# Gates of the latents with seven products for eight, 512-wide conditioning sums and more gates made ahead, in a two-layer mixer trunk

## The chip, the cores and the metric

The kernel runs on one core of a Trainium2 chip. A time is the device time of one execution in microseconds (us). It is given as the median of repeated executions; one more execution is profiled. In the profile PE is TensorE (PEld its weight loads), DVE is VectorE, ACT is ScalarE, POOL is GpSimd and SP is SyncE, which issues the DMAs here.

## The reference

Two layers work on 1024 latent tokens and 256 context tokens of width 1024. Each layer modulates its input by a conditioning vector, projects it to 5632 columns, runs three token mixers (Fourier, gating unit, windowed attention), and merges their projections with sigmoid gates. The last 3072 columns of the projection are the gates.

```python
s_c = jax.nn.silu(c)
for l in range(DEPTH):
    shift, scale, gate = jnp.split(s_c @ w_ada[l] + b_ada[l], 3, axis=-1)
    h = _rms(x) * (1.0 + scale[:, None, :]) + shift[:, None, :]
    fa, za, u, vs, zb, q, k, va, zc, g = _split_proj(h @ w_in[l])
    ...
    ya = _fourier(fa) * jax.nn.silu(za)
    yb = _sgu(u, vs, w_s, b_s) * jax.nn.silu(zb)
    yc = attn * jax.nn.silu(zc)
    ga, gb, gc = jnp.split(jax.nn.sigmoid(g), N_BRANCHES, axis=-1)
    merged = ga * (ya @ w_pa) + gb * (yb @ w_pb) + gc * (yc @ w_pc)
    x = x + gate[:, None, :] * (merged @ w_out[l])
```

Context tokens go through the same steps with a conditioning vector of their own. In the second layer only their keys and values are needed, so there the gates exist for the latents alone. All data is float32.

## The kernel before

**Numbers.** Every float32 operand of a product is split into a high part, rounded to the matmul's format by ScalarE, and a low part, the rest, taken by VectorE. A product is then three matmuls: high by high, high by low, low by high (`mm3`). Operands lie channels on partitions, tokens or columns along the free dimension. `granule` loads a weight tile of up to 128x1024 (`raw`, two buffers) and makes its halves `whi` and `wlo` (five buffers each), one operation of ScalarE (L212) and one of VectorE (L213) per tile.

**Groups.** Tokens are in three groups: "C" (256 of the context), "0" and "1" (512 latents each). `H[g]` holds the layer's modulated input of a group, as eight k blocks of 128 channels with high and low part.

**Stages.** Per layer: attention, Fourier mixing, the gating unit (`sgu`), the gates, the output projection. Projections that do not depend on a stage run in it as fillers (`Fill`), so that TensorE has work: `products` makes the branch projections by `w_pa` and `w_pc` and stages them to DRAM (`S["P", ...]`), and `ahead` makes some gate blocks early and stages their tanh to DRAM (`S["T", ...]`).

**Gates.** `gates` goes through eight column blocks j of 128. For each branch b and group g it multiplies the 128 columns of the gate weights with `H[g]` over all eight k blocks (24 matmuls of 128x512), takes the tanh on ScalarE (L734, into one of the two `ta` buffers), and merges: VectorE computes (tanh + 1) times the branch's projection (L681 for the first branch, L684 for the others, into one of two `tb` buffers), and GpSimd adds it to the column's sum `m` (L685). The branch projection comes from DRAM through `lp`, or, for the middle branch, straight from PSUM: the products by `w_pb` are made here. Merged columns go to DRAM and come back as operands of the output projection.

**Conditioning sums.** The products of the conditioning vectors with `w_ada` for the gate columns of this layer and for the next layer run on VectorE in the gates stage (`ada_dve`): for each item of 256 columns, eight k blocks and one or two vectors, a multiply-add over 128x256 (L196, the first one L192), and at the end small matmuls with a column of ones. `keep_in_program_order` holds the first of them in place.

**Order.** Each engine works through its own list in order. A scheduler makes the lists from the program; the order in which the program is written is a priority, and buffers (`bufs=`) set how far one step can run ahead of another.

## Time and profile before

| | |
|---|---|
| median of three executions | 1948.63 us (1947.56 to 1950.77) |
| profiled execution | 1947.46 us |
| its span, first to last instruction | 1945.7 us |
| mean granted TensorE clock | 0.992 |
| TensorE busy | 1888.2 us, 97% |
| VectorE, ScalarE, GpSimd busy | 1083.1, 798.4, 610.6 us |
| stage of the gates, layer 0 and layer 1 | about 690 to 985 and 1630 to 1858 us |

The span is less than the time of the execution, because starting and ending lie around it. Rows of the profile give a line of the program, the engine, the operation, the tiles it writes and reads (out<-in), and the shape. A row with [.. <-X] tells how long the engine idled before it and what ended the wait. In a table of stretches each engine has its busy time and its count of instructions; in a row of waits stand the total, the number and the longest.

### The profile page before, as it was taken

To read this page: it belongs to the slowest core of one execution; us is meant where nothing else is said; L and a number is where in the kernel's file an instruction comes from. 1 tells how busy PE (TensorE), PEld (TensorE's weight loads), DVE (VectorE), ACT (ScalarE), POOL (GpSimd) and SP (SyncE) were. 2 spreads that over 40 slices of the span, in tenths; PEclk is the share of its full clock that TensorE was granted. 3 is DMA by queue.
4 is the path that set the end of the run, shared out by engine and by line. 5 is a ranking of instruction groups with operands and counts; after the bars stand their busy time and mean duration, and the time that the engine had idled before them with its cause. 6 is when DMAs were issued, how large, how long until landed. Compare 5 with 4: busy or idle time off the path is not lost.

```text
span 1945.7 us, 31000 instructions
## 1 busy us (share of the span) xinstructions
PE 1888.2 (97%) x10975; PEld 1639.1 (84%) x10975; DVE 1083.1 (56%) x2175; ACT 798.4 (41%) x2088; POOL 610.6 (31%) x975
## 2 busy tenths in 40 slices
PE   7889999999999999999999989999999999999998
PEld 2888999999988887888878978899888888888887
DVE  4565665556655548766355556666665655622242
ACT  2654555445644422111243445555554443111221
POOL 1564344443231112121124454334432021211122
PEclk9999999999999999999999999999999999999999
DMA  9332122213554667554374412112124568633362
GB/s 331 105 101 64 50 68 61 72 47 95 162 185 152 191 214 244 164 171 148 120 259 152 136 55 66 57 59 84 34 87 152 155 194 264 201 93 98 127 220 103
DMA packets 270610, 259.77 MB, mean 134 GB/s; under 512 B 20792, under 2 KB 213496, under 8 KB 270456
## 3 DMA queue, kind: packets, MB, share of 16 engines
q1 hardware_dynamic: 270456, 257.80, 41.9%
q8 instruction: 86, 1.41, 0.3%
q14 instruction: 68, 0.56, 0.1%
HBM read 196.91 MB, written 60.83 MB: 132 GB/s over the span
## 4 chain that ended last, share of the span: by engine, by line
PE 82%; DMA 6%; DVE 5%; ACT 3%; issue 2%; POOL 2%; SPq 1%; POOLq 0%; ACTq 0%; DVEq 0%
PE mm L237 16%; PE mm L238 16%; PE mm L239 16%; PE s L238 6%; PE s L237 6%; PE s L239 6%; PE pt L399 3%; DMA raw<-in_w_in_dram 2%; PE o L407 2%; PE o L406 2%; PE s L371 2%; PE s L364 1%; PE s L365 1%; DVE wlo L213 1%; DMA lt<-dT 1%
## 5 line engine op out<-in xcount | busy, mean ns | idle before, releaser
L213 DVE TENSOR_TENSOR wlo<-raw,whi 128x1024 fp32r<-128x1024 f32 (+2 forms) x210 | 243.3, 1161 | 216.3 <-ACT whi L212 207.5
L212 ACT CAST whi<-raw 128x1024 fp32r<-128x1024 f32 (+2 forms) x210 | 202.7, 967 | 363.7 <-PE s L238 139.2
L237 PE MATMUL mm<-hh,whi 128*128 128x512 f32 (+1 forms) x752 | 292.4, 389 | 5.6 <-DVE st L562 3.8
L238 PE MATMUL mm<-hl,whi 128*128 128x512 f32 (+1 forms) x752 | 291.1, 387 | 0.0
L239 PE MATMUL mm<-hh,wlo 128*128 128x512 f32 (+1 forms) x752 | 290.7, 387 | 0.0
L237 PE MATMUL mm<-whi,hh 128*128 128x256 f32 (+1 forms) x704 | 217.6, 309 | 8.1 <-DVE qt L447 5.2
L685 POOL TENSOR_TENSOR m<-m,tb 128x512 f32<-128x512 f32 x64 | 87.1, 1363 | 412.0 <-DVE tb L684 367.6
L239 PE MATMUL mm<-whi,hl 128*128 128x256 f32 (+1 forms) x704 | 214.7, 305 | 0.0
L238 PE MATMUL mm<-wlo,hh 128*128 128x256 f32 (+1 forms) x704 | 214.7, 305 | 0.0
L237 PEld LDWEIGHTS mm<-hh,whi 128*128 128x128 f32 x752 | 141.3, 188 | 33.3 <-DVE st L562 4.7
L239 PEld LDWEIGHTS mm<-hh,wlo 128*128 128x128 f32 x752 | 141.3, 188 | 27.3
L238 PEld LDWEIGHTS mm<-hl,whi 128*128 128x128 f32 x752 | 141.4, 188 | 25.6
L237 PEld LDWEIGHTS mm<-whi,hh 128*128 128x128 f32 x704 | 135.5, 192 | 14.7 <-issue 5.6
L387 POOL TENSOR_SCALAR P<-P,rd 128x640 f32<-128x640 f32 (+2 forms) x144 | 115.0, 809 | 102.1 <-DVE rd L385 63.9
L238 PEld LDWEIGHTS mm<-wlo,hh 128*128 128x128 f32 x704 | 135.7, 193 | 5.0
L239 PEld LDWEIGHTS mm<-whi,hl 128*128 128x128 f32 x704 | 135.4, 192 | 4.8
L238 PE MATMUL s<-hl,whi 128*128 128x512 f32 x352 | 137.5, 391 | 0.0
L237 PE MATMUL s<-hh,whi 128*128 128x512 f32 x352 | 137.4, 390 | 0.0
L239 PE MATMUL s<-hh,wlo 128*128 128x512 f32 x352 | 137.2, 390 | 0.0
L269 DVE TENSOR_TENSOR pl<-pt,ph 128x512 fp32r<-128x512 f32 (+1 forms) x184 | 112.0, 615 | 27.4 <-ACT ph L268 25.0
L268 ACT CAST ph<-pt 128x512 fp32r<-128x512 f32 (+1 forms) x184 | 95.8, 535 | 28.0 <-PE o L406 15.8
L196 DVE SCALAR_TENSOR_TENSOR aacc<-araw,scol,aacc 128x256 f32<-128x256 f32 x196 | 102.2, 554 | 5.1 <-DMA araw<-in_w_ada_dram 2.7
(303 smaller groups left out, 4435.0 us busy)
## 6 DMA issues: line engine op xcount, KB each, us to landing
raw<-in_w_in_dram SPq DMA_DIRECT2D x122, 512.0 KB, 4.1
araw<-in_w_ada_dram SPq DMA_DIRECT2D x48, 512.0 KB, 6.0
raw<-in_w_out_dram SPq DMA_DIRECT2D x40, 512.0 KB, 3.8
dP<-st SPq DMA_DIRECT2D x64, 256.0 KB, 2.3
lp<-dP SPq DMA_DIRECT2D x64, 256.0 KB, 4.2
x<-in_x_dram SPq DMA_DIRECT2D x16, 512.0 KB, 8.6
raw<-in_w_pc_dram SPq DMA_DIRECT2D x32, 256.0 KB, 2.9
dM<-m SPq DMA_DIRECT2D x32, 256.0 KB, 3.4
```

Source lines behind the costliest of these rows:

```text
L196: DVE.scalar_tensor_tensor(acc[:, v, :], raws[k // 4][:, k % 4, :], sc, acc[:, v, :], ALU.mult, ALU.add)
L212: ACT.copy(hi, raw)
L213: DVE.tensor_tensor(lo, raw, hi.bitcast(F32), ALU.subtract)
L237: PE.matmul(o, lh, rh, start=start, stop=False)
L238: PE.matmul(o, lh, rl, start=False, stop=False)
L239: PE.matmul(o, ll, rh, start=False, stop=stop)
L268: ACT.copy(hi, src)
L269: DVE.tensor_tensor(lo, src, hi.bitcast(F32), ALU.subtract)
L371: PE.matmul(bc[:, h * 256:h * 256 + 256], qt[:, s, 2 * pr + h, :], kk[:, g, SEQ:NTOK], start=(h + s == 0), stop=(s == 1), skip_group_check ...
L387: POOL.tensor_scalar(P[hh][:, :nl + 256], P[hh][:, :nl + 256], rd[:, hh:hh + 1], 1.0, ALU.mult, ALU.mult)
L399: PE.transpose(b[:, (2 * i + hh) * 128:(2 * i + hh + 1) * 128], P[hh][:, (i0 + i) * 128:(i0 + i + 1) * 128], ident)
L685: POOL.tensor_tensor(m, m, s, ALU.add)
```

## The change

**Seven products for eight.** For each pair of columns j = 2p, 2p+1 and branch b, the gates of both latent groups are a 2x2 block product: the weights in two k halves by two columns (a11, a12 for the first column, a21, a22 for the second), the inputs in two k halves by two token groups (B11, B21 for "0", T1's source and B22 for "1"). The code takes seven half-k products of 12 matmuls with combinations of the weights (s1 to s4) and of the inputs (T1 to T4), and sums them in PSUM where that is possible; x2, x3, x5 are partial results that ScalarE copies out. s1 is made by VectorE, s2 to s4 by GpSimd (L757), one late sum by VectorE (L828), another by GpSimd (L840). 18 pairs are made so, ten in layer 0 and eight in layer 1.

**Differences.** T1 to T4 are made once per layer (`differences`), ahead of the gates, T1 in the place of B12. The fillers beside them are four late gate blocks and the products by `w_pb`, which now go to DRAM too.

**Merging.** It reads the branch projections of all three branches from DRAM. The context's two columns are merged as one tile of 512; all of the context's merged columns go to DRAM. The order of the output groups in layer 0 is "0", "C", "1".

**Conditioning sums.** `ada_steps` works on one k block of 512 columns at a time. The layer's own gate columns are summed under the gating unit, the next layer's in layer 0's gates, one step after each of the first products.

**Casts.** `operand` makes halves of 512 columns from a raw tile that is always 1024 wide (ten buffers each).

**Gates ahead.** Eight blocks in layer 0 and sixteen in layer 1 are made ahead of their merging, where before it was four and eight.

```diff
-    def ada_dve(l, jb, nv, pool):
...
+    def ada_steps(items, pool):
...
+        def block(l, jb, nv, k, acc):
+            raw = pool.tile([128, 512], F32, "araw", bufs=2)
+            nc.sync.dma_start(raw, a["w_ada"][l, k * 128:(k + 1) * 128, jb * 128:jb * 128 + 512])
+
+            def sums():
+                if k == 0:
+                    acc.extend(tb() for _ in range(nv))
                 for v in range(nv):
                     sc = scol[:, k, v:v + 1]
                     if k == 0:
+                        ins = DVE.tensor_scalar(acc[v], raw, sc, None, ALU.mult)
                     else:
+                        ins = DVE.scalar_tensor_tensor(acc[v], raw, sc, acc[v], ALU.mult, ALU.add)
+                    if v == 0:
+                        tc.keep_in_program_order(ins)
...
+    def operand(src, n=512):
+
+        hi = wp.tile([128, 512], F32R, "whi", bufs=10)[:, :n]
+        lo = wp.tile([128, 512], F32R, "wlo", bufs=10)[:, :n]
+        ACT.copy(hi, src)
+        DVE.tensor_tensor(lo, src, hi.bitcast(F32), ALU.subtract)
+        return hi, lo
...
+    def differences(tpool):
...
+        def steps():
+            for k in range(KC // 2):
+                for t, x, y in ((T3, B22, B12), (B12, B12, B11), (T2, B22, B12), (T4, B21, T2)):
+                    d = ta()
+                    POOL.tensor_tensor(d, x[0][k].bitcast(F32), y[0][k].bitcast(F32), ALU.subtract)
+                    e = tb()
+                    DVE.tensor_tensor(e, x[1][k].bitcast(F32), y[1][k].bitcast(F32), ALU.subtract)
+                    DVE.tensor_tensor(d, d, e, ALU.add)
+                    split(t[0][k], t[1][k], d)
+                    yield
...
+        def times(o, A, B, start):
+            for k in range(KC // 2):
...
+                PE.matmul(o, A[0][:, c], B[0][k], start=start and k == 0, stop=False, skip_group_check=True)
+                PE.matmul(o, A[0][:, c], B[1][k], start=False, stop=False, skip_group_check=True)
+                PE.matmul(o, A[1][:, c], B[0][k], start=False, stop=last, skip_group_check=True)
+            next(sums, None)
...
+        def add(m, b, t, pp):
             if b == 0:
                 DVE.scalar_tensor_tensor(m, t, 1.0, pp, ALU.add, ALU.mult)
             else:
-                s = tb(n)
-                DVE.scalar_tensor_tensor(s, t, 1.0, pp, ALU.add, ALU.mult)
-                POOL.tensor_tensor(m, m, s, ALU.add)
...
+                DVE.scalar_tensor_tensor(pp, t, 1.0, pp, ALU.add, ALU.mult)
+                POOL.tensor_tensor(m, m, pp, ALU.add)
...
+                if ("T", b, js[0], "0") in S:
+                    for g in lat:
+                        for j in js:
+                            t = ta()
+                            nc.sync.dma_start(t, S["T", b, j, g])
+                            merge(j, g, t, True)
+                    continue
...
+                A = operand(a11)
+                times(z, A, B11, True)
+                ACT.copy(x, z)
+                s1 = combined(DVE, a21, a22, ALU.add)
+                A = operand(s1)
+                times(y, A, T1, True)
+                x5 = copy("x5", y)
+                s2 = combined(POOL, s1, a11, ALU.subtract)
+                A = operand(s2)
+                times(z, A, T2, False)
+                x2 = copy("x2", z)
+                A = operand(a12)
+                times(x, A, B21, False)
...
+                s4 = combined(POOL, a12, s2, ALU.subtract)
+                s3 = combined(POOL, a11, a21, ALU.subtract)
...
+                times(z, A, T3, False)
+                x3 = copy("x3", z)
+
+                def p3():
+                    A = operand(s4)
+                    times(y, A, B22, False)
+                    DVE.tensor_tensor(x2, y, x2, ALU.add)
+                    merge(js[0], "1", x2)
+
+                def p4():
+                    A = operand(a22)
+                    times(z, A, T4, False)
...
+                POOL.tensor_tensor(x3, x3, x5, ALU.add)
+                merge(js[1], "1", x3)
...
-        blocks = [(b, 0, g) for b in (0, 2) for g in lat]
+        pairs = [(b, p) for p in range(2 if last else 1) for b in (0, 2)]
+        blocks = [(b, 2 * p + i, "1") for b, p in pairs for i in range(2)]
+        late = [(b, j, "0") for b, j, _ in blocks[-4:]]
...
+        sums = ada_steps(ada, sp)
         for i, _ in enumerate(sgu(l, groups, sp, S, yb)):
+            for x in range(2):
+                next(sums, None)
+                fill.upto((i + (x + 1) / 2) * whole / (units // 128))
...
+        sevens, combos = differences(tpool)
+        fill = Fill(ahead(l, late[:2], S, st), products(l, groups, yb, 2, "w_pb", 1, S, st, True), ahead(l, late[2:], S, st))
+        for i, _ in enumerate(combos):
+            fill.upto((i + 1) * (16 * units + 2048) / 16)
+        fill.rest()
...
+        gates(l, groups, S, [] if last else [(l + 1, j, 2) for j in (8, 0, 12, 4)], A, sevens)
```

**The order on VectorE.** The scheduler's list for VectorE inside layer 0's gates, before the change (L196 and L192 are the sums, L213 a low half of weights, L269 one of `w_pb`, L684 a merge):

```order
L192 TENSOR_SCALAR aacc_9346<-araw,scol 128x256 x2
L196 SCALAR_TENSOR_TENSOR aacc_9346<-araw,scol,aacc_9346 128x256 x3
L684 SCALAR_TENSOR_TENSOR tb<-ta,pt 128x512
L684 SCALAR_TENSOR_TENSOR tb<-ta,lp_9484 128x512
L196 SCALAR_TENSOR_TENSOR aacc_9346<-araw,scol,aacc_9346 128x256
L269 TENSOR_TENSOR pl<-praw,ph 128x512
L196 SCALAR_TENSOR_TENSOR aacc_9346<-araw,scol,aacc_9346 128x256 x6
L213 TENSOR_TENSOR wlo<-raw,whi 128x1024
```

And after it, around the combination s1 (L757) of the fourth pair (L193 are the sums, L223 low halves, L762 and L764 merges, L828 the late sum x2):

```order
L762 SCALAR_TENSOR_TENSOR m_10243<-x_10392,lp 128x512
L193 SCALAR_TENSOR_TENSOR tb<-araw,scol,tb 128x512
L757 TENSOR_TENSOR sw<-raw 128x512
L193 SCALAR_TENSOR_TENSOR tb<-araw,scol,tb 128x512
L762 SCALAR_TENSOR_TENSOR m_10242<-ta,lp 128x512
L193 SCALAR_TENSOR_TENSOR tb<-araw,scol,tb 128x512
L764 SCALAR_TENSOR_TENSOR lp<-ta,lp 128x512
L223 TENSOR_TENSOR wlo<-sw,whi 128x512
L193 SCALAR_TENSOR_TENSOR tb<-araw,scol,tb 128x512
L828 TENSOR_TENSOR x_10531<-s,x_10531 128x512
```

Between the making of s1 and its low half, which is the operand of the second product, the list now has two sums and two merges, and the merges take their tanh and projection from tiles in SBUF.

**The order on GpSimd.** Before the change, its list in the same stage holds only the additions of the merging:

```order
L685 TENSOR_TENSOR mC<-mC,tb 128x256 x2
L685 TENSOR_TENSOR m_9107<-m_9107,tb 128x512
L685 TENSOR_TENSOR m_9108<-m_9108,tb 128x512
L685 TENSOR_TENSOR m_9107<-m_9107,tb 128x512
L685 TENSOR_TENSOR m_9108<-m_9108,tb 128x512
```

After it (L757 are s2, s4 and s3, L840 is x3, L765 the additions of the merging):

```order
L757 TENSOR_TENSOR sw<-sw,raw 128x512
L765 TENSOR_TENSOR m_9973<-m_9973,lp 128x512
L757 TENSOR_TENSOR sw<-raw,sw 128x512
L765 TENSOR_TENSOR m_9974<-m_9974,lp 128x512
L757 TENSOR_TENSOR sw<-raw 128x512
L765 TENSOR_TENSOR m_9975<-m_9975,lp 128x512
L840 TENSOR_TENSOR x_10392<-x_10392,x_10302 128x512
```

The combinations that TensorE's operands are made from now alternate with the additions, in one list.

More of the change, by code (lines that the diff above doesn't have):

```diff
@@ new lines, in sums @@
+                    if v == 0:
+                        tc.keep_in_program_order(ins)
+                if k == KC - 1:
+                    pa = bank("o")
+                    for i in range(4):
+                        for v in range(nv):
+                            PE.matmul(pa[:, 2 * i + v:2 * i + v + 1], acc[v][:, i * 128:(i + 1) * 128], ones[:, 0:1], start=True, stop=True)
+                    for i in range(4):
+                        DVE.tensor_scalar(adac[l][:, jb + i, 0:nv], pa[:, 2 * i:2 * i + nv], bada[l][:, jb + i:jb + i + 1], None, ALU.add)
@@ new lines, in block @@
+            return sums
+        for l, jb, nv in items:
+            acc = []
+            for k in range(KC):
+                if len(todo) == 2:
+                    todo.pop(0)()
+                todo.append(block(l, jb, nv, k, acc))
+                yield
+        for f in todo:
+            f()
+            yield
+    def operand(src, n=512):
[4 more added lines that the diff above has]
+        return hi, lo
@@ new lines, in raw_weights, with part @@
+    def raw_weights(src, shape):
+        raw = wp.tile([128, 1024], F32, "raw", bufs=2)
+        n = shape[1] * shape[2]
+        nc.sync.dma_start(raw[:, :n].rearrange("p (k c) -> p k c", k=shape[1]), src)
+        return raw[:, :n]
+    def granule(src, shape):
+        raw = raw_weights(src, shape)
+        n = shape[1] * shape[2]
+        return [operand(raw[:, c:min(c + 512, n)], min(512, n - c)) for c in range(0, n, 512)]
+    def part(w, width, k, c0=0, n=None):
+        c = k * width + c0
+        x = c // 512
+        c -= x * 512
+        return [y[:, c:c + (n or width)] for y in w[x]]
@@ L615, in gated_u @@
                     yield 2 * n
-        lead = context_blocks(range(9, 12)) if "C" in groups else [(b, 2, "0") for b in (0, 2)]
+        lead = context_blocks(range(9, 12)) if "C" in groups else [(2, j, "0") for j in range(2)]
         return ([ahead(l, lead, S, st), silus("Z", C_ZC, (2, 3)), silus("A", C_ZA, (0, 1))] + [rows(l, groups, "F", C_FA, S, st)],
@@ L624, in before_work @@
             return ahead(l, context_blocks(range(9)), S, st)
-        return ahead(l, [(b, 1, "0") for b in (0, 2)], S, st, CTX)
+        return ahead(l, [(0, j, "0") for j in range(2)], S, st, CTX)
     def few(gen, n):
@@ L669, in products, with half_blocks, new @@
                 yield n * nkb
-    def gates(l, groups, S, ada, side, yb):
-        mp = Pool(tc, name="mp", bufs=1, side=side)
-        zq = Pool(tc, name="zq", bufs=1, side=side)
-        lat = [g for g in groups if g != "C"]
-        hC = new_h("C") if "C" in groups else None
-        todo = []
-        def add(m, b, t, n, pp):
+    def half_blocks(g, i):
+        return [H[g][x][4 * i:4 * i + 4] for x in range(2)]
+    def differences(tpool):
+        def new(tag):
+            ts = [tpool.tile([128, KC // 2, 512], F32R, f"{tag}{x}") for x in "hl"]
+            return [[t[:, k, :] for k in range(KC // 2)] for t in ts]
+        B11, B12, B21, B22 = (half_blocks(g, i) for i in range(2) for g in ("0", "1"))
+        T2, T3, T4 = new("t2"), new("t3"), new("t4")
+        def steps():
[7 more added lines that the diff above has]
+                    split(t[0][k], t[1][k], d)
+                    yield
+        return (B11, B21, B22, B12, T2, T3, T4), steps()
@@ L743, in gates @@
+        for k in (KC - 2, KC - 1):
+            merged("0", k, mp, "araw", 2)
         mp.close()
@@ L922, in out_phase @@
         wt[0] = w_half(a["w_out"][l], 0)
-        if order[0] != "C":
-            operands(order[0])
+        operands(order[0])
         load(order[0])
@@ L983, in trunk_kernel @@
         groups = ["0", "1"] if last else ["C", "0", "1"]
-        ada = [(l, j, 1 if last else 2) for j in range(16, 24, 2)]
-        if not last:
-            ada += [(l + 1, j, 2) for j in range(0, 16, 2)]
+        ada = [(l, j, 1 if last else 2) for j in (16, 20)]
         S = {}
```

208 lines of the change are left out of this document (98 added, 110 removed).

## The prediction

> **What bounds the kernel now.** I read the page's first and fourth parts, then a table of stretches, then the two timelines that show VectorE and GpSimd next to each other, and the waits.
>
> ```profile
> span 1945.7 us, 31000 instructions
> PE 1888.2 (97%) x10975; PEld 1639.1 (84%) x10975; DVE 1083.1 (56%) x2175; ACT 798.4 (41%) x2088; POOL 610.6 (31%) x975
> PE 82%; DMA 6%; DVE 5%; ACT 3%; issue 2%; POOL 2%; SPq 1%; POOLq 0%; ACTq 0%; DVEq 0%
> ```
>
> TensorE is busy 97% of the span and carries 82% of the chain that ended last: matmuls bound the kernel, and whatever takes matmuls away pays, as long as nothing else rises above what is left. The profiled execution took 1947.46 us, 1.76 more than its span and 0.06% under the median of the runs, 1948.63. Whether something else rises is a question for the stages that are edited. Of the stretches below, the columns are the bounds in us, the length, then busy time and count of PE, PEld, DVE, ACT and POOL, the granted clock, the DMA share and GB/s. In order they are layer 0's gating unit with the products of `w_pa`, layer 0's gates, the same two of layer 1, 100 us inside the last, and 3.4 us that the clock argument needs.
>
> ```profile
> core 0: us, PE busy (x) PEld busy (x) DVE busy (x) ACT busy (x) POOL busy (x), PEclk, DMA share, GB/s
> 616.00:690.00 74.00, 70.68 (x347) 58.71 (x347) 42.67 (x76) 33.64 (x77) 17.28 (x30) 0.98 0.63 195
> 690.00:985.00 295.00, 292.44 (x1359) 242.61 (x1358) 184.43 (x344) 66.55 (x102) 56.53 (x48) 1.00 0.58 178
> 1545.00:1630.00 85.00, 83.37 (x381) 67.67 (x380) 44.66 (x71) 36.19 (x73) 13.69 (x24) 1.00 0.62 194
> 1630.00:1858.00 228.00, 227.27 (x1007) 187.44 (x1006) 93.75 (x128) 54.75 (x80) 43.49 (x32) 1.00 0.49 155
> 1750.00:1850.00 100.00, 100.00 (x442) 82.58 (x441) 26.71 (x34) 23.25 (x34) 13.74 (x11) 1.00 0.35 113
> 628.70:632.10 3.40, 3.40 (x10) 2.43 (x10) 3.40 (x7) 2.44 (x5) 1.73 (x3) 0.50 0.50 150
> ```
>
> The fifth gives the price of a matmul: 100.00 / 442 = 0.226 us from start to start for 128x512. A product of 12 (half of k, three matmuls each) is 2.71 us, the seven of a pair 19.0. In the first four rows PE idles 3.3, 2.6, 1.6 and 0.7 us, 8.2 in all. In layer 0's gates VectorE and GpSimd are busy 184 + 57 us of 295. That looks like room, but the two timelines show that they don't run side by side.
>
> ```profile
> 735.10 1.78 DVE L681 SCALAR_TENSOR_TENSOR m<-ta,lp 128x512 f32<-128x512 f32 x1
> 736.80 0.68 DVE L684 SCALAR_TENSOR_TENSOR tb<-lt,lp 128x512 f32<-128x512 f32 x1
> 737.40 0.47 DVE L196 SCALAR_TENSOR_TENSOR aacc<-araw,scol,aacc 128x256 f32<-128x256 f32 x1
> 737.80 1.77 DVE L681 SCALAR_TENSOR_TENSOR m<-ta,lp 128x512 f32<-128x512 f32 x1
> 750.83 0.68 DVE L684 SCALAR_TENSOR_TENSOR tb<-ta,lp 128x512 f32<-128x512 f32 x1
> 751.43 1.52 DVE L196 SCALAR_TENSOR_TENSOR aacc<-araw,scol,aacc 128x256 f32<-128x256 f32 x1
> 752.88 1.77 DVE L269 TENSOR_TENSOR pl<-praw,ph 128x512 fp32r<-128x512 f32 x1
> ```
>
> And GpSimd's of the same stretch:
>
> ```profile
> 735.00 1.33 POOL L685 TENSOR_TENSOR m<-m,tb 128x512 f32<-128x512 f32 x1 [3.02 <-DVE tb L684]
> 737.56 1.46 POOL L685 TENSOR_TENSOR m<-m,tb 128x512 f32<-128x512 f32 x1 [1.23 <-DVE tb L684]
> 750.99 3.11 POOL L685 TENSOR_TENSOR m<-m,tb 128x512 f32<-128x512 f32 x2 [3.85 <-DVE tb L684]
> ```
>
> The merge begun on VectorE at 735.10 ends at 736.88, 0.55 after GpSimd's addition ended (735.00 + 1.33 = 736.33); the next one ends at 739.57, again 0.55 after GpSimd (739.02). Undisturbed such an operation takes 0.68 and its successor starts 0.60 later (736.80 to 737.40). In the other direction GpSimd's pair from 750.99 waits for the VectorE operation that ends at 751.51, runs, lets the sum end at 752.95, and ends its second addition at 754.10, 1.15 later. So operations with two SBUF operands on the two engines take turns: 0.58 for one of VectorE (between 0.55 and 0.60), 1.15 for one of GpSimd, added up. That sum is the second clock of this kernel, and the change works on it.
>
> **The change, part by part.**
>
> Products. 18 pairs (ten in layer 0, eight in layer 1) drop 12 matmuls each: 216 x 0.226 = **-48.9 us**. The PE program shrinks by 11,117 - 10,901 = 216, so the change does what it says, and every other product is only moved. The two stages' idle time is replaced by what follows: **-8.2**.
>
> Differences. Before the pairs come 16 steps, each a GpSimd subtraction and three VectorE operations. They begin when the sums let go of the two `tb` buffers. From there on VectorE issues 49 two-operand operations and GpSimd 14: 49 x 0.58 + 14 x 1.15 = 44.5 us, against 44.3 us of products made ahead and of `w_pb`, which are the cover. Alone that costs nothing; without this cover it would cost the 44.5. But it enters the gates with no slack.
>
> Layer 0's pairs. I counted the operations that VectorE and GpSimd issue up to the last operand that can hold PE back, which is s4 of the seventh pair. Beside the differences there are 91 two-operand operations of VectorE (the low halves, L757, the merges) at 0.58, 56 sums 512 wide and 46 of GpSimd. The sums' price is in the start of the program:
>
> ```profile
> L160 DVE SCALAR_TENSOR_TENSOR aacc<-araw,scol,aacc 128x512 f32<-128x512 f32 x14 | 9.6, 732 | 0.0
> L192 DVE TENSOR_SCALAR aacc<-araw,scol 128x256 f32<-128x256 f32 x28 | 9.9, 369 | 0.4 <-DMA araw<-in_w_ada_dram 0.4
> L684 DVE SCALAR_TENSOR_TENSOR tb<-ta,pt 128x512 f32<-128x512 f32 x32 | 21.8, 681 | 22.0 <-ACT ta L734 20.6 <-PE pt L239 1.4
> L665 ACT COPY st<-mm 128x512 f32<-128x512 f32 x32 | 18.6, 582 | 24.0 <-PE mm L239 20.3 <-issue 3.7
> L212 ACT CAST whi<-raw 128x512 fp32r<-128x512 f32 x40 | 24.5, 618 | 38.1 <-PE mm L238 18.7 <-DMA raw<-in_w_pc_dram 9.8 <-DMA raw<-in_w_pa_dram 7.0
> ```
>
> 9.6 / 14 = 0.69 each. For the eight first steps, twice the width of L192's rows, I take 0.5 (between 0.37 and 0.69), and 3.1 us for all the rest. So 52.8 + 38.6 + 4.0 + 3.1 + 52.9 = 151.4, of which 1.7 lie behind that operand. From the start of the differences the port is needed for 44.5 + 149.7 = 194.2 us, and after that operand 24 products are left on PE, 65.1 us: 259.3. PE alone needs 44.3 + 70 x 2.71 = 234.3. With a port that is never idle PE waits 25.0 us here. How well it is packed decides the rest. At 735 to 741 it is taken without a gap. Against that stand the waits for loads:
>
> ```profile
> DVE mC L681 <- DMA lt<-dT_C: 20.3, 7, 6.2
> L681 DVE SCALAR_TENSOR_TENSOR mC<-lt,lp 128x256 f32<-128x256 f32 x8 | 3.4, 424 | 20.3 <-DMA lt<-dT_C 20.3
> lp<-dP SPq DMA_DIRECT2D x64, 256.0 KB, 4.2
> ```
>
> Seven of eight such merges waited, 20.3 / 7 = 2.9 us each, with VectorE's whole queue behind it; the merges are issued in one order with the low halves that PE waits for. I take six such waits in the 194 us, 17 us: 8% lost, 194.2 / 0.92 = 211.1, and 211.1 + 65.1 - 234.3 = **+42**. No wait gives 25, twelve (15% lost) give 59.
>
> Layer 1's pairs have no sums: differences 39.3 against 43.6 us of cover; pairs of 10 to 21, in the mean 15.4, against 19.0. Fully packed this costs 0, at 85% 11; at 92% **+2**.
>
> Sums of the layer's own gate columns. They go under layer 0's gating unit, where VectorE was busy 42.67 of 74 us (58%). 28 at 0.69 and 4 at 0.5 make 21 us on the 37 us of PE work that they are spread over, which holds 0.58 x 37 = 21 already: 42 against 37, **+5** (0 if they fit the gaps, 14 if the idle stretches can't be used). In layer 1 they are one vector, half of that, on 53%: 0.
>
> Casts. 448 pieces of 512 replace 168 of 1024 and 40 of 512, 72 pieces more (72 x 0.6 = 43 us on each of two engines over two layers). ScalarE does 7 casts, 4 copies and some 4 tanh a pair, 15 x 0.6 = 9 of 19 us: nothing, since it stands idle half of the time; VectorE's share is in the counts above. The context's merging, moved to half as many operations twice as wide, is also in them. The first output group starts on six of eight k: 0.
>
> The sum: 1945.7 - 48.9 - 8.2 + 42 + 2 + 5 = 1937.6 of span, and 1.8 outside: **1939 us**, 0.5% faster. Of 57 us saved, the port takes back 49.
>
> **The rivals.**
>
> R1, the port doesn't bind. The order in which VectorE serves operands could let PE run its other products first, and sums, which nobody waits for soon, fall behind. Then 1945.7 - 48.9 - 8.2 + 5 + 1.8 = 1895. For it: only s2, s3 and s4 are on GpSimd. Against: the sums stand in VectorE's order ahead of low halves, and the 194 us lie on the port whatever the order.
>
> R2, slower: the loads of finished gates hold VectorE. In layer 0 twenty merges (twelve of the context, eight of gates made ahead) wait for loads through two `ta` and three `lp` buffers. A buffer comes free only when VectorE or GpSimd has read it, so the load starts late. At 2.9 us each that is 58 us instead of the 17 above: 1939 + 41 = 1980. It decides from the point at which PE's waits exceed 57 us. For it: the seven waits of eight. Against: four merges in a pair of 19 us give a load that runs two buffers ahead some 9 us, and loads of this size landed in 4.2.
>
> R3, the clock. A wait of PE is followed by a slow stretch:
>
> ```profile
> 626.93 0.39 PE L883 MATMUL pt<-wsh,vh 128*128 128x256 f32 x1 [2.23 <-ACT vh L878]
> ```
>
> After 2.23 us of waiting the clock was 0.50 from 628.70 to 632.10 (in the stretches above), 1.7 us lost. If every pair has such a wait, those in the port-bound stretch lose nothing, since PE waits there anyway, and the other twelve lose 20 us: 1959. Against: most waits forecast here are of 0.5 to 2 us, and PE's share stays above 80%. The Trainium skill, "TensorE: Matmul & The Clock Gate", in "A second HAM failure mode: psum-queue depth-cycling", tells of a kernel where small PE idles between groups of matmuls, with PSUM banks in turn, made the clock oscillate; by that rule R3 would be the likelier. This trace agrees only in part: in layer 0's gates PE is held up for 2.6 us in all, banks change with every product, and the granted clock is 1.00; so R3 keeps a small chance.
>
> **How the numbers follow.** The forecast (port-bound, partly packed) has 0.60, R1 0.14, R2 0.18, R3 0.08. The likeliest case's own range goes from 25 and 0 and 0 for its three costs (1915) to 54, 4 and 5 with 13% of the port's time lost (1953). The whole range, 1905 to 1975, leaves out most of R1 and the upper half of R2, some 0.20. A measurement here can tell 0.2%, 3.9 us, from no change: faster is under 1944.7. Of the forecast's 0.60, 0.46 lie there, 0.08 within and 0.06 above. With R1 that makes faster 0.60; with a little of R3, same 0.10; the rest, slower 0.30.
>
> **What would show it.** Right: the first pairs of layer 0's gates take 19 to 30 us each with PE idle 10 to 25%, waiting for low halves (L223) whose release came from GpSimd's L757 or VectorE; VectorE's operations there last 1.7 where GpSimd is at work; layer 1's pairs take 19 to 20. Matmuls 0.226 as before. Wrong: PE busy over 97% in layer 0's gates (R1), merges waiting 2 us and more for `ta` or `lp` in most pairs (R2), a granted clock under 0.97 there (R3), or a gating unit in layer 0 where PE idles for more than 15 us.

## The result and the profile after

The changed kernel takes 2013.45 us (median of four executions, 2005.95 to 2018.42), the kernel before 1948.62: a ratio of 1.033, with a 95% interval of 1.030 to 1.035. It is slower by 65 us, where some 10 us of gain were forecast, and lies above the forecast's range. The profiled execution is the fastest of the four, 2005.95 us with a span of 2004.2, 66.6 more than the span that the prediction summed up to. One execution below is left out, of the last kernel with eight products: it took 3783.58 us, and as it is the one that was profiled, no table of that kernel is shown.

The head of its page, with the row of the granted clock:

```profile
span 2004.2 us, 31840 instructions
PE 1885.8 (94%) x10759; PEld 1619.2 (81%) x10759; DVE 1311.4 (65%) x2415; ACT 926.4 (46%) x2464; POOL 796.1 (40%) x1071
PEclk9999999999999999889999999999999999999999
```

TensorE's records are 216 fewer, as the order said, but its busy time fell by only 2.4 us, where 18 pairs save 48.9: the matmuls that are left became slower. The clock row shows where it was most (two slices at 8), and the mean granted clock is 0.975 after 0.992. Now stretches of the same kernel. In order: layer 0's gating unit; the rest of the sums and of the products by `w_pa`, and the differences; the gates; 100 us within them; layer 1's differences and gates; the two output stages. The columns are those of the prediction's table.

```profile
616.00:665.00 49.00, 45.73 (x217) 37.98 (x216) 31.79 (x58) 25.33 (x61) 11.87 (x22) 0.97 0.63 197
665.00:774.00 109.00, 89.51 (x414) 70.54 (x413) 80.49 (x119) 35.34 (x70) 32.47 (x24) 0.95 0.71 161
774.00:1020.00 246.00, 223.53 (x926) 179.32 (x925) 201.32 (x241) 89.58 (x163) 123.42 (x78) 0.92 0.63 196
800.00:900.00 100.00, 87.15 (x345) 69.97 (x344) 97.95 (x115) 32.31 (x59) 58.51 (x35) 0.85 0.67 203
1648.00:1724.00 76.00, 66.13 (x275) 51.47 (x274) 60.05 (x87) 27.65 (x52) 28.82 (x21) 0.96 0.67 182
1724.00:1910.00 186.00, 170.22 (x695) 134.89 (x694) 135.04 (x140) 76.31 (x137) 100.99 (x65) 0.95 0.56 179
1020.00:1138.00 118.00, 113.78 (x512) 92.09 (x511) 75.64 (x107) 54.68 (x99) 42.80 (x42) 0.99 0.62 219
1910.00:2004.00 94.00, 84.63 (x365) 69.01 (x363) 37.24 (x49) 19.90 (x33) 23.95 (x17) 0.97 0.51 181
```

A stretch loses time in two ways, and both are read here: idle time (length less PE's busy time) and slow clock (one less the clock, times the length). Layer 0's gates lose 22.5 + 0.08 x 246 = 42 us, layer 1's 15.8 + 9.3 = 25, the differences 19.5 + 5.5 = 25 and 9.9 + 3.0 = 13. What TensorE waited for, six rows of the answer for its waits (total, times, longest):

```profile
PE mm L268 <- ACT st L695: 19.0, 12, 6.6
PE s L745 <- ACT whi L222: 10.5, 4, 5.0
PE mm L268 <- DVE st L697: 8.9, 9, 2.4
PE mm L745 <- ACT pt L800: 8.7, 5, 5.2
PE s L747 <- DVE wlo L223: 6.3, 3, 4.1
PE mm L745 <- ACT x L752: 4.9, 4, 2.6
```

The first and the third row lie almost wholly in the two stretches ahead of the gates (19.0 and 8.5 us there): products of `w_pa` and `w_pb` (L268 to L270) wait for a bank to be emptied into a staging tile, the longest, 6.6 us, in the differences. The others lie in the gates (L745 to L747 are the seven products), in many places: high halves, low halves and copies. Counting those over 0.3 us, TensorE waits 13 times in layer 0's gates and six times in layer 1's, at most 5.2 and 5.0 us. And this is what VectorE and GpSimd do there: 18 us of layer 1's gates as a row, then eight of them in the timelines, VectorE first:

```profile
1749.00:1767.00 18.00, 16.32 (x68) 12.57 (x68) 17.19 (x13) 7.23 (x13) 16.88 (x10) 0.97 0.48 140
```

```profile
1749.81 1.67 DVE L223 TENSOR_TENSOR wlo<-sw,whi 128x512 fp32r<-128x512 f32 x1
1751.39 3.48 DVE L764 SCALAR_TENSOR_TENSOR lp<-ta,lp 128x512 f32<-128x512 f32 x2
1754.80 1.78 DVE L223 TENSOR_TENSOR wlo<-sw,whi 128x512 fp32r<-128x512 f32 x1
1756.50 1.78 DVE L223 TENSOR_TENSOR wlo<-raw,whi 128x512 fp32r<-128x512 f32 x1
```

and GpSimd:

```profile
1750.88 1.74 POOL L765 TENSOR_TENSOR m<-m,lp 128x512 f32<-128x512 f32 x1
1752.58 1.74 POOL L757 TENSOR_TENSOR sw<-raw,sw 128x512 f32<-128x512 f32 x1
1754.29 1.75 POOL L840 TENSOR_TENSOR x<-x,x 128x512 f32<-128x512 f32 x1
1755.99 3.45 POOL L765 TENSOR_TENSOR m<-m,lp 128x512 f32<-128x512 f32 x2
```

One of each every 1.70 us, strictly in turn: 1.15 + 0.55, the prices of the prediction. The Trainium skill, "SBUF — State Buffer", in "SBUF: two separate sides", calls the port pair that the two engines share an exclusive lock, held for a whole instruction; the rows agree, with 1.74 us for an addition that takes 1.29 where VectorE stands idle (25 of the 64 in the kernel before). TensorE, though, idles for only 1.7 us of these 18. Where the turns cost most is in layer 0: between 800 and 900 us VectorE is busy for 97.95 us with 115 operations, which at the undisturbed 0.60 to 0.69 would take 69 to 79 (an estimate from these prices).

### The profile page after: what moved, and what is told of

Its sections match the earlier page's. It is cut to its first block, busy times and chain, and to the rows that moved or that the text cites. A ratio compares the mean times of both kernels' runs of the same rounds, so it can differ in the third digit from the quotient of the medians.

```text
span 2004.2 us, 31840 instructions
## 1 busy us (share of the span) xinstructions
PE 1885.8 (94%) x10759; PEld 1619.2 (81%) x10759; DVE 1311.4 (65%) x2415; ACT 926.4 (46%) x2464; POOL 796.1 (40%) x1071
## 4 chain that ended last, share of the span: by engine, by line
PE 35%; DVE 10%; DMA 8%; issue 4%; POOL 2%; ACT 2%; SPq 1%; POOLq 0%; DVEq 0%; ACTq 0%
PE mm L268 6%; PE mm L269 6%; PE mm L270 6%; DVE wlo L223 3%; DMA raw<-in_w_in_dram 2%; DVE tb L193 2%; PE s L269 2%; PE s L268 2%; PE s L270 2%; PE pt L429 1%; DMA araw<-in_w_ada_dram 1%; DVE lp L764 1%; DMA raw<-in_w_out_dram 1%; PE mm L745 1%; PE mm L746 1%
## 5 line engine op out<-in xcount | busy, mean ns | idle before, releaser
L223 DVE TENSOR_TENSOR wlo<-raw,whi 128x512 fp32r<-128x512 f32 x378 | 286.7, 771 | 170.4 <-ACT whi L222 158.1
L222 ACT CAST whi<-raw 128x512 fp32r<-128x512 f32 x378 | 229.2, 620 | 298.7 <-PE mm L269 115.8
L268 PE MATMUL mm<-whi,hh 128*128 128x256 f32 (+1 forms) x704 | 216.7, 308 | 5.7 <-DVE qt L477 2.8
L270 PE MATMUL mm<-whi,hl 128*128 128x256 f32 (+1 forms) x704 | 215.4, 306 | 0.0
L269 PE MATMUL mm<-wlo,hh 128*128 128x256 f32 (+1 forms) x704 | 214.4, 304 | 0.0
L268 PE MATMUL mm<-hh,whi 128*128 128x512 f32 (+1 forms) x528 | 205.4, 389 | 6.2 <-ACT st L695 2.2
L269 PE MATMUL mm<-hl,whi 128*128 128x512 f32 (+1 forms) x528 | 204.7, 388 | 0.0
L270 PE MATMUL mm<-hh,wlo 128*128 128x512 f32 (+1 forms) x528 | 204.1, 386 | 0.0
L268 PEld LDWEIGHTS mm<-whi,hh 128*128 128x128 f32 x704 | 135.5, 192 | 12.3 <-issue 3.1
L270 PEld LDWEIGHTS mm<-whi,hl 128*128 128x128 f32 x704 | 135.3, 192 | 5.5 <-DVE hl L322 0.5
L269 PEld LDWEIGHTS mm<-wlo,hh 128*128 128x128 f32 x704 | 135.5, 192 | 5.2
L765 POOL TENSOR_TENSOR m<-m,lp 128x512 f32<-128x512 f32 x64 | 101.6, 1590 | 94.0 <-DVE lp L764 94.0
L268 PEld LDWEIGHTS mm<-hh,whi 128*128 128x128 f32 x528 | 99.8, 189 | 26.1 <-ACT st L695 3.2
L270 PEld LDWEIGHTS mm<-hh,wlo 128*128 128x128 f32 x528 | 99.8, 189 | 18.7
L269 PEld LDWEIGHTS mm<-hl,whi 128*128 128x128 f32 x528 | 99.7, 189 | 17.3
L193 DVE SCALAR_TENSOR_TENSOR tb<-araw,scol,tb 128x512 f32<-128x512 f32 x98 | 92.7, 970 | 8.5 <-DMA araw<-in_w_ada_dram 8.1
L429 PE MATMUL pt<-ident,P 128*128 128x128 f32 x640 | 97.3, 272 | 0.0
L1049 POOL TENSOR_TENSOR x<-x,og 128x512 f32<-128x512 f32 x36 | 50.8, 1422 | 116.7 <-DVE og L1047 80.6
L222 ACT CAST whi<-sw 128x512 fp32r<-128x512 f32 x72 | 43.3, 619 | 113.0 <-DVE sw L757 57.8
```

What stands on the lines that cost most here:

```text
L193: ins = DVE.scalar_tensor_tensor(acc[v], raw, sc, acc[v], ALU.mult, ALU.add)
L222: ACT.copy(hi, src)
L223: DVE.tensor_tensor(lo, src, hi.bitcast(F32), ALU.subtract)
L268: PE.matmul(o, lh, rh, start=start, stop=False)
L269: PE.matmul(o, lh, rl, start=False, stop=False)
L270: PE.matmul(o, ll, rh, start=False, stop=stop)
```

## The experiments

Each kernel was timed beside the kernel before, whose medians lay between 1947 and 1949.5. Besides the port (operations of VectorE and GpSimd taking turns, as forecast) two rivals were formed from the trace of the change. **Chain**: the path of one operand through ScalarE, VectorE and GpSimd sets the pace. **DMA**: a narrow DMA that came into the differences holds up the other transfers. Every edit is made in the changed kernel, unless something else is said. An edit lets the scheduler make new lists, so some microseconds of each difference may come from that (4.5 in one of the controls below).

**GpSimd's operations of the gates on VectorE.**

```diff
-                POOL.tensor_tensor(m, m, pp, ALU.add)
+                DVE.tensor_tensor(m, m, pp, ALU.add)
...
-                s2 = combined(POOL, s1, a11, ALU.subtract)
+                s2 = combined(DVE, s1, a11, ALU.subtract)
```

(and the same for s3, s4 and x3)

> The changed kernel, with all of GpSimd's operations in the gates (s2, s3, s4, x3 and the additions of the merging) on VectorE, so that no turn is lost between the two: each costs 0.60 in place of 1.15. Theory port: layer 0 needs 46 x 0.55 = 25 us less of the port up to the seventh pair, so its gates get 25 to 40 us shorter, layer 1's, which have no sums, at most 5: 1970 to 1985. Theory chain: what shortens is the path of s2 to s4, about 1 us a pair in both layers alike, and VectorE's list gets longer: 1995 to 2005, with layer 1 gaining as much per pair as layer 0.

It took 1963.71 us, ratio 1.008 (1.006 to 1.009): 50 us less than the change, more than the forecast of the port. Of its table the gates of the two layers, and the price of the merging's addition in the change and here:

```profile
775.00:994.00 219.00, 208.49 (x930) 168.22 (x930) 191.14 (x323) 92.62 (x165) 0.00 (x0) 1.00 0.70 222
1698.00:1867.00 169.00, 162.61 (x696) 131.23 (x695) 128.84 (x203) 76.57 (x137) 2.33 (x2) 0.99 0.62 198
```

```profile
L765 POOL TENSOR_TENSOR m<-m,lp 128x512 f32<-128x512 f32 x64 | 101.6, 1590 | 94.0 <-DVE lp L764 94.0
```

```profile
L765 DVE TENSOR_TENSOR m<-m,lp 128x512 f32<-128x512 f32 x64 | 43.9, 689 | 0.4
```

Layer 0's gates fell from 246 to 219 us (27, inside the port's forecast), layer 1's from 186 to 169 (17, where the port was given at most 5). For each pair that is 2.7 and 2.1 us: the size is over what the chain was given (1 us), but layers that gain nearly alike are the chain's sign, not the port's. VectorE does 82 operations more in layer 0 and is busy for 10 us less. The slow clock went with the waits: 1.00 and 0.99 after 0.92 and 0.95.

**Only the additions.** The same edit for `m` and x3, with s2, s3 and s4 left on GpSimd.

> The changed kernel (2013 us) with only the additions of the merging (64) and x3 (18) on VectorE; s2, s3 and s4 (54 operations), from which TensorE's operands are made, stay on GpSimd. With all 136 moved it took 1964, 50 less. Theory port: what counts is how many operations take turns, so 82 of 136 bring 30 of the 50: about 1983. Theory chain: what counts is the path of an operand, and the three combinations on it stay where they were: 2000 or more.

1982.95 us, ratio 1.018 (1.016 to 1.021): 30.5 of the 50 us for 82 of the 136 operations, what the port was given to the microsecond. The combinations that TensorE's operands are made from were not moved. So the gain goes with the number of operations moved and not with the operands' path, in layer 1 too. One rival is not separated by this: the additions also stood in GpSimd's list between the combinations, and waited there 94 us in all for VectorE's merges (the row above), so moving them clears that list as well as sparing turns. The gates of the two layers:

```profile
776.00:1006.00 230.00, 215.04 (x926) 173.11 (x925) 198.52 (x290) 91.04 (x164) 56.38 (x30) 0.96 0.67 210
1709.00:1887.00 178.00, 165.32 (x695) 131.46 (x694) 137.00 (x179) 76.60 (x137) 40.52 (x26) 0.98 0.60 187
```

**The sums left out.**

```diff
-                for v in range(nv):
+                for v in range(nv if k == 0 or jb >= 16 else 0):
```

This leaves out seven of eight k blocks of the next layer's conditioning, so layer 1 computes with other numbers.

> The changed kernel without the next layer's conditioning sums in layer 0's gates: of eight k blocks only the first is multiplied (56 operations of 128x512 on VectorE are left out; the loads stay). So layer 1 works with wrong conditioning numbers. Theory port: 56 x 0.66 = 37 us less on the port up to the seventh pair, and layer 0's gates lose 25 to 37 us: 1976 to 1988. Theory chain: the sums only stand between other operations, 5 to 12 us: 2001 to 2008. Nothing in layer 1 changes by either.

1996.59 us, ratio 1.025 (1.023 to 1.026): 17 us less. Layer 0's gates went from 246 to 232; 37 us were taken from the port and 14 came out. The result lies between the two forecasts; that the sums fill gaps as well as standing in the way would explain it and is not shown.

**The differences on VectorE.** The subtraction of L718 is issued on VectorE.

> The changed kernel, with the 32 subtractions of the differences on VectorE in place of GpSimd. Theory port: 0.55 less for each, 9 us in a layer, but the stage has as much matmul work beside it: 2005 to 2013. Theory chain: a k block of differences took 13.6 us because the four steps follow one another through two buffers, each with a GpSimd operation of 1.7 and a VectorE operation that ends 0.55 behind it; on VectorE it takes some 9 to 10, and the stage's waits go: 1985 to 2000.

2000.90 us, ratio 1.027 (1.025 to 1.029): 12.5 less, between the two ranges, nearer to the chain's.

**The differences' loops exchanged.**

```diff
-            for k in range(KC // 2):
-                for t, x, y in ((T3, B22, B12), (B12, B12, B11), (T2, B22, B12), (T4, B21, T2)):
+            for t, x, y in ((T3, B22, B12), (B12, B12, B11), (T2, B22, B12), (T4, B21, T2)):
+                for k in range(KC // 2):
```

> The changed kernel with the two loops of the differences exchanged: the same 16 steps, but all four k blocks of one step before the next step, so that no step follows directly on the one whose result it reads. Theory chain: a k block took 13.6 us, since three of its four steps wait for one another (subtraction, addition, cast, low half, 4.6 us each); exchanged, the stage is set by the turns of the two engines, and its 14 us of excess in each layer go for the most part: 1988 to 2000. Theory port: the same operations take the same turns: 2008 to 2014.

2005.32 us, ratio 1.030 (1.028 to 1.033): 8 us less, less than the chain was given (13 to 25), and with intervals that overlap. The last subtraction came 13 us earlier in the profile (755.4 after 768.6 us), the first of the seven products only 5 (769.3 after 774.1). So something else held the stage by then.

**The narrow DMA held back.** The output stage needs the layer's gate column as a row. A DMA of 1024 elements turns it; with the sums now under the gating unit, its data is ready at 713 us, and SyncE issues it at once. Held back, it is issued in the gates:

```diff
+            if p == 2:
+                for v in range(2 if "C" in groups else 1):
+                    row = S["gate", v] = dp.tile([KC, 128], F32, f"gate{l}{v}")
+                    tc.keep_in_program_order(nc.sync.dma_start(row.rearrange("j p -> p j"), adac[l][:, 16:24, v]))
```

> The changed kernel (2013 us), but the narrow DMA that lays the layer's gate column out as a row (1024 elements of 4 bytes, issued at 713 us in the trace of the changed kernel, in the middle of the differences, and at 1688 in layer 1) is held back on SyncE until the third pair of columns in the gates. Theory DMA: while it ran, loads landed after 17 us and stores after 14, and TensorE stood for staging tiles to come free (6.6 us at 727, 4.2 at 1696); the stage of the differences loses 10 to 18 us of its waits over both layers: 1995 to 2003. Theory port (VectorE and GpSimd taking turns sets the pace) and theory chain (the path of one operand through ScalarE, VectorE and GpSimd in their orders): 2010 to 2013, the waits are only filled with others.

2009.07 us, ratio 1.032 (1.030 to 1.034): 4 us less with overlapping intervals: far from the 10 to 18 that the DMA was given for being held back. What the DMA does in the change is in these answers: SyncE's timeline (L675 is a store of tanh), and for 712 to 728 us the packets and the landings (KB each, us).

```profile
713.00 0.37 SPq L1010 DMA_DIRECT2D gate<-adac  x1
713.48 0.52 SPq L675 DMA_DIRECT2D dT<-st  x1
714.05 0.43 SPq L1010 DMA_DIRECT2D gate<-adac  x1
```

```profile
DMA packets 2892, 0.61 MB, mean 38 GB/s; under 512 B 2096, under 2 KB 2764, under 8 KB 2892
dT<-st SPq DMA_DIRECT2D x2, 256.0 KB, 14.5
raw<-in_w_in_dram SPq DMA_DIRECT2D x1, 512.0 KB, 17.0
gate<-adac SPq DMA_DIRECT2D x2, 4.0 KB, 13.9
```

And ScalarE and TensorE behind it:

```profile
725.25 0.37 ACT L695 COPY st<-mm 128x256 f32<-128x256 f32 x1 [2.78 <-DMA dT<-st]
733.30 1.07 ACT L695 COPY st<-mm 128x512 f32<-128x512 f32 x2 [6.64 <-DMA dT<-st]
733.94 0.58 PE L268 MATMUL mm<-ybhC,whi 128*128 128x256 f32 x1 [6.60 <-ACT st L695]
```

Two times 4 KB took 14 us, in 2048 elements of 4 bytes, beside which the window has few other packets under 512 bytes (2096 in all); a store of 256 KB took 14.5, its staging tile stayed taken, ScalarE waited 6.6 us for the tile and TensorE for ScalarE. In the median of the whole run such a store took 2.4 and such a load 4.2:

```profile
dP<-st SPq DMA_DIRECT2D x96, 256.0 KB, 2.4
raw<-in_w_in_dram SPq DMA_DIRECT2D x126, 512.0 KB, 4.2
```

**Three edits together.** GpSimd's operations of gates and differences on VectorE, the loops exchanged; and the same with the DMA held back.

> The changed kernel with GpSimd's operations of the gates and of the differences on VectorE and the loops of the differences exchanged. If the three add up: 2013 - 50 - 12 - 15 = 1936. If the differences' waits have a common cause in the narrow DMA or in the staging tiles, the last two bring no more than one of them: 1950.

> As the run before it in this list, with the narrow DMA of the gate column held back until the third pair of columns. Theory DMA: with nothing else slow in the differences the DMA shows in full, 8 to 15 us less. Otherwise within 3 us of the run before.

1952.37 us (ratio 1.003, 1.001 to 1.004) and 1950.14 (1.002, 1.001 to 1.003). The three don't add up to 1936; they end near the 1950 of a common cause. Holding the DMA back moved 2 us. In its profile the stage ahead of the gates got shorter by 7 us in layer 0 (760.7 after 767.9 us), and in the gates TensorE waited 3.8 us from 854 and 4.7 from 1761, where the DMA ran now (issued at 847 and 1751, landed after 11.6 and 10.5). So it seems to cost wherever loads and stores are wanted.

**The row made by a transpose.** TensorE transposes the column, ScalarE copies it, and a DMA of eight pieces of 512 bytes writes it.

```diff
...
+                    pr = bank("o")
+                    PE.transpose(pr[0:KC, 0:128], adac[l][:, 16:24, v], ident)
+                    rs = ta(128)
+                    ACT.copy(rs[0:KC, :], pr[0:KC, 0:128])
+                    nc.sync.dma_start(row, rs[0:KC, :])
...
```

> The changed kernel (2013 us) with only the row made by a transpose, as in the run before it in this list. Theory DMA: 8 to 15 us less, 1998 to 2005, whatever the port does. Theory port: GpSimd and VectorE set the pace behind it, and at most 5 us show: 2008 to 2013.

> As the kernel with all of GpSimd's operations of the gates and the differences on VectorE and the loops exchanged (1952 us), but the gate column becomes a row by a transpose on TensorE, a copy on ScalarE and a DMA of eight pieces of 512 bytes, in the third pair of the gates, in place of 1024 pieces of 4 bytes. Held back to the same place, the narrow DMA took TensorE's time there instead (waits of 4.0 us at 853 and 4.9 at 1761) and the whole moved 2 us. Theory DMA: the narrow pieces themselves cost the 8 us or so that the differences win without them, wherever they stand; without them 1940 to 1946. If the waits have other causes and only move: 1949 to 1953.

Alone it took 1992.43 us (ratio 1.023, 1.022 to 1.025), 21 less than the change and more than was given to it; with the three other edits 1933.20 (ratio 0.993, 0.991 to 0.995), 19 less than without it and 7 under the forecast. Here the DMA theory is shown: the narrow pieces cost some 20 us, since the same edit with narrow pieces in the same place (held back) took off 4 and 2. All together turn the change into a gain of 0.7% over the kernel before. That isn't the worth of the change alone: the kernel before gains too, 7 us, from one of these edits (the controls), and with a transposed row it was not tried. Its own narrow DMA runs at 790 and 1694 us, in gates that idle 2.6 and 0.7 us in all, so there is little to win there.

Of the 21 us some 14 come off the differences, 10 in layer 0 and 4 in layer 1. Their rows with the transposed row alone lose 14 and 9 us:

```profile
665.00:764.00 99.00, 86.57 (x409) 68.29 (x408) 78.20 (x117) 35.06 (x69) 31.90 (x22) 0.98 0.53 175
1637.00:1709.00 72.00, 64.76 (x278) 50.99 (x278) 59.12 (x87) 27.36 (x52) 29.08 (x21) 0.98 0.56 190
```

The table of the kernel with all four edits, called the mended kernel below, for the same stages from the gating unit of layer 0 to the gates of layer 1:

```profile
616.00:666.00 50.00, 46.63 (x233) 39.05 (x232) 32.22 (x59) 26.60 (x62) 11.94 (x22) 1.00 0.66 205
666.00:759.00 93.00, 85.23 (x415) 68.10 (x414) 77.85 (x136) 35.02 (x70) 5.72 (x8) 1.00 0.58 191
759.00:977.00 218.00, 209.26 (x932) 169.32 (x931) 189.84 (x320) 92.14 (x167) 0.00 (x0) 0.99 0.70 222
1606.00:1671.00 65.00, 61.62 (x276) 49.77 (x277) 58.01 (x104) 27.64 (x50) 2.21 (x3) 1.00 0.61 206
1671.00:1835.00 164.00, 160.76 (x693) 129.50 (x692) 125.61 (x201) 76.23 (x137) 0.00 (x0) 1.00 0.64 203
```

The differences lose 7.8 and 3.4 us in place of 25 and 13, the gates 11 and 3 in place of 42 and 25.

**Eight products again.** Over the same pieces, with no differences and no combinations; the sums of conditioning, the gates ahead, the staging stay. Once in the change, and once with the additions on VectorE and the row by a transpose.

```diff
-                s1 = combined(DVE, a21, a22, ALU.add)
-                A = operand(s1)
-                times(y, A, T1, True)
...
+                        for i in range(2):
+                            times(o, W[j][i], B[g, i], i == 0)
```

> The changed kernel (2013 us) with eight products of 12 matmuls a pair again, over the same 512-wide pieces, and no differences and no combinations of weights: the sums, the gates made ahead, the staging, the narrow DMA and the additions on GpSimd stay as in the change. 216 matmuls more (+48.9 us); 32 steps of differences and 126 combinations, copies' sums and so on of VectorE and GpSimd fewer. Theory port: the turns that made TensorE wait are those of the seven products; without them its waits in the gates and ahead of them fall to about 20 us in place of some 110, and the kernel takes 1950 to 1970, less than with seven. If the rest of the change (sums, DMA, staging) made the waits: 2020 or more.

> As the run before it in this list, with the additions of the merging on VectorE and the gate column made a row by a transpose; beside the kernel with the same and seven products (1933 us) it is the net worth of the seven. If the 48.9 us of matmuls come in full: 1982. With what the differences and combinations still cost there (some 30 us of waits ahead of the gates and in them): 1940 to 1955. If seven is not worth it at all: 1933 or less.

1982.16 us (ratio 1.017, 1.015 to 1.018) and 1966.06 (median of five; 1.009, 1.007 to 1.011). So in the change as it was made, seven products cost 31 us more than eight, and in the mended kernel some 33 us less. No forecast had either number: both lie between the values that were given. With eight products the other parts of the change still cost 33 us. The table of the first kernel shows where: its gates lose 20.3 + 0.05 x 297 = 35 us in layer 0, and 1.0 us in layer 1.

```profile
722.00:1019.00 297.00, 276.73 (x1211) 228.02 (x1211) 130.85 (x191) 66.58 (x119) 56.51 (x39) 0.95 0.60 184
1680.00:1887.00 207.00, 205.96 (x912) 170.30 (x912) 65.23 (x95) 53.87 (x93) 43.24 (x31) 1.00 0.59 182
```

So a loss of the size of layer 0's 42 us stands there without any pair of seven. VectorE and GpSimd are busy there 131 and 57 us of 297, so over the stage the port isn't full. TensorE waits five times: 9.1 us for low halves, 7.1 for the conditioning sums and 4.0 for a tanh. The first of these, from VectorE's timeline and TensorE's:

```profile
732.18 0.69 DVE L755 SCALAR_TENSOR_TENSOR m<-ta,lp 128x512 f32<-128x512 f32 x1 [12.24 <-DMA ta<-dT]
733.53 0.79 PE L740 MATMUL s<-hh,wlo 128*128 128x512 f32 x1 [5.31 <-DVE wlo L223]
```

A merge waited 12.2 us for the load of a finished gate, and the low half stood behind the merge. SyncE issued that load only at 729.60 us, after the store of the same tanh had landed, which took 12.6 us beside the narrow DMA of 714.8. That is the mechanism of R2, set off by the DMA. It is read from the trace, and no run takes it away by itself.

**Controls.** The kernel before with its 64 additions on VectorE; the mended kernel with the first multiplication of each conditioning sum on ScalarE; the mended kernel with four buffers for the combinations.

> The kernel before (1947 us) with its 64 additions of the merging on VectorE in place of GpSimd: the same edit that took 30 us off the changed kernel, together with x3. Theory port: VectorE and GpSimd were never late for TensorE in the gates of that kernel (2.6 and 0.7 us of idle time), so the turns cost it nothing: 1944 to 1949. If the edit helps for another reason (GpSimd as such), it gains here too: 1935 or less.

> As the first run of this list, with the first multiplication of each conditioning sum (14 of 112) on ScalarE instead of VectorE. If VectorE's list is what still holds TensorE back in layer 0, 14 x 0.4 = 6 us come off it, 1 to 5 us of the time; if ScalarE's list does (it makes the casts), the time gets 1 to 5 us longer.

> The fastest kernel so far (1933 us) with four buffers for the combinations of weights in place of two. If the waits that are left in its gates come from bursts (combinations of one pair have to wait until the last ones are used up): 1920 to 1928. If VectorE's time as such does it: 1931 to 1936.

The first took 1941.81 us (ratio 0.997, 0.995 to 0.998), 7 less than the kernel before and 2 under the port's range. In its profile the last product of layer 0's gating unit comes 4.5 us earlier, ahead of any operation that the edit touches, so at least that much is the new list; a real but small cost of GpSimd before the change is not excluded. The second took 1936.41 us (0.994, 0.992 to 0.995), no different from 1933. The third took 1947.59 (0.999, 0.998 to 1.000), 14 more than with two buffers and outside both forecasts: the scheduler uses them to make s3 and s4 earlier, ahead of merges and low halves on VectorE. That the earlier combinations are the cause was not tested; that 14 us go with this edit is measured.

## Why the prediction was wrong

It named a resource that binds and its price rightly, and the sum wrongly. By its own steps:

- **Products, -48.9.** The change does leave out the 216 matmuls. Their net worth is some 33 us once the rest is out of the way (1966 against 1933), and less than nothing before.
- **Layer 0's pairs, +42.** The number is right, 42 measured, and the operations on GpSimd bring back 27 of it. That it fits so well is partly luck. Nearly half of it came as slow clock, 19.7 us, which the step didn't contain, and only 22.5 as idle time; and with eight products the same stage lost 35 us, by other waits. Idle time and slow clock can't be told apart further here: a slow clock in a stretch that waits anyway costs nothing, and both went when GpSimd's operations were moved. Of R3 the half is right: PE did wait, and the clock did fall, to 0.85 between 800 and 900 us; its sign, a clock under 0.97, was there. In the trace of the change the gates have ten stretches at half clock, of 3.4 to 13.7 us, and eight of them begin during a single wait of 1.6 to 5.2 us or within 2 us of its end. With GpSimd's operations on VectorE, nine waits of 0.5 to 1.7 us in layer 0's gates came with no such stretch. The Trainium skill, "TensorE: Matmul & The Clock Gate", in "A second HAM failure mode: psum-queue depth-cycling", tells of small idles between groups of matmuls that are frequent enough to make the clock oscillate; the traces agree only in that the clock fell where TensorE waited often, and small idles alone did not do it here.
- **Layer 1's pairs, +2.** Wrong by 23. This is the first step that failed: "pairs of 10 to 21, in the mean 15.4, against 19.0", with 92% of the port's time used. Eight pairs of 15.4 are 123 us on 152 us of products. Counted in the trace, the stage of 186 us has 132 operations of VectorE with two SBUF operands and 65 of GpSimd, at the prediction's prices 151 us, on 695 matmuls of 0.226, 157 us. So all that runs there needs the port nearly as long as TensorE works, and it was packed to 151 of 186 us, 81%; the same count for layer 0, with the sums at their own price, gives 220 of 246, 89%. At 92% the 151 us would have cost 7. That GpSimd's operations cost this is shown by the 17 us that came back without them, and by the 30.5 for 82 of 136 operations over both layers. How they hold TensorE up in layer 1 is not shown: the longest wait there, 5.0 us from 1727, lies behind the last differences in VectorE's list, and where the port is full (1749 to 1767) TensorE idles for 1.7 us.
- **Differences, 0.** Wrong by 25 and 13, and the second step that failed. "44.5 us, against 44.3 us of products" compared amounts only. The cover itself needed ScalarE, staging tiles and stores, and none of the three was named as what would be late. Without the narrow DMA they lose 14 and 9, so it accounts for 10 and 4; with the subtractions on VectorE and the loops exchanged as well they lose 7.8 and 3.4. Which of these two edits brings how much there is open: alone they took 12.5 and 8 us off the whole.
- **Sums under the gating unit, +5.** The stretch of 616 to 665 us loses 3.3 of idle time and 1.5 of clock, as much as before the change; what comes of it is the narrow DMA, which follows on the last sum. The prediction counted the operations that were moved and not the DMA that their result releases.
- **Casts, output groups, 0.** The output stages idle 4.2 and 9.4 us, 7 us more than the 1.1 and 5.2 of before in the rows below, with 3.9 us among them in which TensorE waited for VectorE's first operation on the output (L1047), which itself waited 2.0 us for the read of the gate row. It was not looked at further.

```profile
985.00:1098.00 113.00, 111.86 (x519) 91.95 (x518) 59.41 (x68) 43.88 (x59) 39.90 (x40) 1.00 0.55 185
1858.00:1945.00 87.00, 81.84 (x362) 67.45 (x360) 25.60 (x29) 12.22 (x12) 20.63 (x16) 0.99 0.45 158
```

- **Sum.** 25 in layer 0's differences, 13 in layer 1's, 23 in its gates, 7 in the output stages, and 2 less under the gating unit (3.3 of idle time, where 5 were put in): 66 of the 66.6 us. The clock is known to two digits, 1 us on a stretch of 200, so that it comes out so closely is chance.
- **R2, loads that hold the merges.** In the change it didn't happen: the waits of merges for `ta` and `lp` come to 14 us in the whole profile, where 17 had been put into the forecast. The largest:

```profile
DVE lp L764 <- DMA ta<-dT_C: 5.9, 2, 3.2
```

What stays open: which of the other parts cost the rest of the 33 us with eight products once the DMA is taken off (the mended one with eight products is still 17 us slower than the kernel before), by what path GpSimd's operations hold TensorE up in layer 1, and how much of the slow clock cost time by itself.

## What to carry to other kernels

Where two engines take turns at a resource, count the demand of everything that runs in the stage, not only of the step that is changed, and don't expect it to be packed: 81 and 89% were reached here. An operation on an idle engine isn't free: 136 of them moved to the busier engine took 50 us off. Of a step that is moved, follow the result too, down to the DMA that it releases, and look at what else uses the queues at the new time. An algorithm with fewer matmuls has to be tried with the rest mended before it is judged; here it went from 31 us worse to some 33 us better than the plain one.

## What was not expected of the hardware

A DMA of 4 KB in 4-byte elements, two of them in 1 us, took 14 us, and ordinary transfers beside it landed after 14.5 and 17 us in place of 2.4 and 4.2; the same row in eight pieces landed in 3.9 to 6.7 together with its read, and 20 us were won. The Trainium skill, "DMA: Bandwidth & Descriptors", in "Rules for kernel authors", says that a last dimension which is not contiguous becomes one descriptor per element and should be rearranged; the 2096 small packets agree. And the granted clock fell to 0.85 over 100 us in which TensorE was still busy 87% of the time, with seven waits of 0.4 to 5.2 us (shorter ones not counted).
